# A two-layer diffusion backbone on one core: the instruction order is made by the framework's timeline simulation

## The chip, the cores and the metric

The kernel runs on one core of a Trainium2 chip. The metric is device time in microseconds (us) from the start to the end of one execution. The core has five engines that matter here, each with its own instruction queue: TensorE (PE; its weight loads are listed as PEld), VectorE (DVE), ScalarE (ACT), GpSimd (POOL) and SyncE (SP), which here only starts DMA transfers. An engine takes its queue in order and waits on semaphores for results of the others.

## What is computed

Two layers over 512 latent tokens and 256 context tokens of width 1024, all in fp32. Each layer has one input projection and three mixers side by side, then a projection back and an MLP:

```
h = rmsnorm(x) * (1 + scale) + shift
q, k, v, a, b, z, u, gate = split(h @ w_in)
o_na = neighbourhood_attention(q, k, v, kc, vc, rpb)     # 8 heads, softmax over window and context
o_dn = gated_head_norm(delta_f + delta_b, z)             # 4 heads, two directions, chunks
o_fn = real(fft2(u))                                     # 4 groups
y = (g_na * (o_na @ w_na_o) + g_dn * (o_dn @ w_dn_o) + g_fn * (o_fn @ w_fn)) @ w_out
x = x + gate1 * y
x = x + gate2 * (relu(rmsnorm(x) ... @ w1) ** 2 @ w2)
```

The delta rule solves a unit lower triangular system per chunk (`triangular_solve(I + strict_lower(beta k k^T * decay), rhs)`) and then carries a 128 x 128 state from chunk to chunk. In layer 1 the context tokens give only keys and values.

## The kernel before

**Stages.** A layer runs in three parts. First come norms, the Fourier mixer and the first delta head's inputs. Then comes the mix stage, in which the input projections, the attention and the delta rule run side by side (180.0 to 760.0 us in layer 0, 1658.8 to 2147.0 us in layer 1). Last comes the main stage: branch products, output projection, MLP (760.0 to 1540.0 us and 2147.0 us to the end); 1540.0 to 1658.8 us is the first part of layer 1.

**Projections.** `proj` (L250 to L256) makes every large product of fp32 weights as three products of halves: high weight with high input, high with low, low with high. All are recorded at L255, in 512 columns (`ps_in`) and 256 columns (`ps_inc`). `wload` (L235 to L248) brings 256 KB of weights (L240, a DMA issued on SP), takes their high half on ACT (L243) and the low half on DVE or POOL (L246); in the mix stages it is always POOL.

**Attention.** For each pair of heads and tile of 128 queries (`na_pair`): scores on PE (L841, L842), maxima, exponentials and sums on DVE and ACT (L806 to L819), the product with the reciprocal sum on DVE (L820), transposes on PE (L825), a copy on ACT (L826), products with V on PE (L831).

**Delta rule.** `l2_rope` (L484 to L507) takes the norm of keys and queries with a product against ones (L492) and turns them; `tok_major` (L509 to L517) transposes them (L515). `dn_prep` (L534 to L658) runs per head: six chunks of key products (L564) and query products (L566) give the tile `N`, whose diagonal blocks go out to DRAM (`nd`, L581, four DMAs) and come back as 48 blocks of 32 x 32 on 48 partitions (`Nb`, L583). Then DVE inverts them in 31 steps of a product (L591) and a subtraction (L593), each on the result of the last. L596 transposes; two DMAs write the result (L598, L599) and eight bring it back into `N` and `Tst` (L602, L603). Block products on PE then make the whole inverse (L612, L622, L638, L643). `dn_step` (L660 to L709) is one chunk of one direction of the recurrence, six per direction and head: L678 and L680 multiply with the state, L683 with the inverse, L685 copies the result on ACT, L687 makes the next state's product (added on DVE, L692), L705 the output's product (added on DVE, L703 to L709). `dn_out` (L720 to L738) norms a head's output (L729 on DVE) and transposes it (L735).

**What sets the order.** The program issues the mix stage through `by_clock`, which takes pieces of four streams (recurrence, `dn_prep`, attention, input projections) by a clock of rough costs and gives them priorities. The tile framework's scheduler then makes one order of all instructions, engine by engine, from the dependencies, the priorities and its own reckoning of times. The order is fixed when the program is built. Buffers limit it: `N`, `L` and the solve's scratch tile have one buffer each, so one head's inverse is in work at a time. The context that holds this scheduler is opened in `kernel` (L1359).

## Time and profile before

| | us |
|---|---|
| median of three timed runs | 2654.89 |
| the three runs | 2654.8, 2654.89, 2670.13 |
| the profiled execution | 2672.64 |
| its span, first to last instruction | 2670.7 |
| PE busy | 2481.4 (93%) |
| PE weight loads busy | 2046.0 (77%) |
| DVE busy | 1599.2 (60%) |
| ACT busy | 1187.1 (44%) |
| POOL busy | 645.8 (24%) |

The mean granted clock of TensorE is 0.974 of full speed. A matmul row's busy time holds its time in the pipe, so a busy share of PE over a stage says less than the spacing of its instructions. A wait is put down to the instruction whose semaphore came last. SPq rows are DMA issues in SP's queue, not transfers; the transfer ends later.

### The profile page before, as it was taken

To read this page: it belongs to the slowest core of one execution; us is meant where nothing else is said; L and a number is where in the kernel's file an instruction comes from. 1 tells how busy PE (TensorE), PEld (TensorE's weight loads), DVE (VectorE), ACT (ScalarE), POOL (GpSimd) and SP (SyncE) were. 2 spreads that over 40 slices of the span, in tenths; PEclk is the share of its full clock that TensorE was granted. 3 is DMA by queue.
4 is the path that set the end of the run, shared out by engine and by line. 5 is a ranking of instruction groups with operands and counts; after the bars stand their busy time and mean duration, and the time that the engine had idled before them with its cause. 6 is when DMAs were issued, how large, how long until landed. Compare 5 with 4: busy or idle time off the path is not lost. (4 is left out here: it accounts for less than half of the span.)

```text
span 2670.7 us, 39375 instructions
## 1 busy us (share of the span) xinstructions
PE 2481.4 (93%) x14608; PEld 2046.0 (77%) x14608; DVE 1599.2 (60%) x3207; ACT 1187.1 (44%) x2453; POOL 645.8 (24%) x536
## 2 busy tenths in 40 slices
PE   6988989899998999999999988888989999999998
PEld 3776877777887878888888867766767777788886
DVE  5647687768556967564434474868768456433334
ACT  4545545565564233131313264556555663423333
POOL 3231212231122122111111133222333232222222
PEclk8999999999999999999999999999989999999999
DMA  6232122222154643434343323223232346232332
GB/s 220 70 82 71 64 59 68 76 82 73 55 180 147 225 142 110 123 111 126 119 126 115 118 62 97 71 69 80 65 79 66 99 131 197 79 95 95 97 97 87
DMA packets 186247, 275.66 MB, mean 103 GB/s; under 512 B 57364, under 2 KB 77592, under 8 KB 185928
## 3 DMA queue, kind: packets, MB, share of 16 engines
q1 hardware_dynamic: 186056, 273.16, 33.8%
q8 instruction: 114, 1.87, 0.3%
q14 instruction: 77, 0.63, 0.1%
HBM read 242.86 MB, written 26.03 MB: 101 GB/s over the span
## 5 line engine op out<-in xcount | busy, mean ns | idle before, releaser
L246 POOL TENSOR_TENSOR wlo<-wr,whi 128x512 fp32r<-128x512 f32 x352 | 493.2, 1403 | 1666.8 <-ACT whi L243 1590.9
L243 ACT CAST whi<-wr 128x512 fp32r<-128x512 f32 x544 | 336.1, 619 | 794.8 <-PE ps_m L255 494.7
L255 PE MATMUL ps_in<-hh,whi 128*128 128x512 f32 x960 | 379.1, 406 | 15.5 <-ACT kraw L761 7.7
L255 PE MATMUL ps_in<-hh,wlo 128*128 128x512 f32 x960 | 375.4, 402 | 1.9 <-POOL wlo L246 1.9
L255 PE MATMUL ps_in<-hl,whi 128*128 128x512 f32 x960 | 376.8, 403 | 0.0
L255 PE MATMUL ps_m<-ml,whi 128*128 128x512 f32 (+1 forms) x768 | 234.2, 359 | 4.1 <-POOL ml L323 3.6
L255 PE MATMUL ps_m<-mh,whi 128*128 128x512 f32 (+1 forms) x768 | 232.2, 357 | 4.7 <-ACT mh L319 4.7
L255 PE MATMUL ps_m<-ah,wlo 128*128 128x512 f32 (+1 forms) x776 | 234.4, 355 | 0.0
L255 PE MATMUL ps_m<-al,whi 128*128 128x512 f32 (+1 forms) x776 | 233.1, 354 | 0.0
L255 PE MATMUL ps_m<-ah,whi 128*128 128x512 f32 (+1 forms) x776 | 233.0, 353 | 0.0
L255 PE MATMUL ps_m<-mh,wlo 128*128 128x512 f32 (+1 forms) x768 | 232.2, 356 | 0.0
L246 DVE TENSOR_TENSOR wlo<-wr,whi 128x512 fp32r<-128x512 f32 x192 | 134.7, 702 | 141.5 <-ACT whi L243 140.9
L255 PEld LDWEIGHTS ps_in<-hh,whi 128*128 128x128 f32 x960 | 181.4, 193 | 48.5 <-ACT kraw L761 8.1
L255 PEld LDWEIGHTS ps_in<-hh,wlo 128*128 128x128 f32 x960 | 180.0, 192 | 35.7 <-POOL wlo L246 3.2
L255 PEld LDWEIGHTS ps_in<-hl,whi 128*128 128x128 f32 x960 | 181.0, 193 | 30.3 <-issue 2.0
L1198 DVE SCALAR_TENSOR_TENSOR x<-ps_m,mod,x 128x512 f32<-128x512 f32 (+1 forms) x97 | 60.8, 654 | 217.9 <-PE ps_m L255 217.9
L202 DVE SCALAR_TENSOR_TENSOR jada<-wada,csb 128x1024 f32<-128x1024 f32 x128 | 179.1, 1399 | 1.2 <-DMA wada<-in_wat_dram 0.7
L255 PE MATMUL ps_inc<-hh,whi 128*128 128x256 f32 x512 | 150.9, 295 | 1.9 <-ACT gl L407 1.9
L255 PEld LDWEIGHTS ps_m<-ml,whi 128*128 128x128 f32 x768 | 127.7, 189 | 29.3 <-POOL ml L323 6.7
L255 PE MATMUL ps_inc<-hh,wlo 128*128 128x256 f32 x512 | 149.9, 293 | 0.0
L255 PE MATMUL ps_inc<-hl,whi 128*128 128x256 f32 x512 | 149.1, 291 | 0.0
L255 PEld LDWEIGHTS ps_m<-mh,whi 128*128 128x128 f32 x768 | 127.3, 189 | 27.7 <-ACT mh L319 6.4
(339 smaller groups left out, 5026.9 us busy)
## 6 DMA issues: line engine op xcount, KB each, us to landing
wr<-in_w_dram SPq DMA_DIRECT2D x256, 256.0 KB
wr<-in_wi_dram SPq DMA_DIRECT2D x224, 256.0 KB
wada<-in_wat_dram SPq DMA_DIRECT2D x80, 512.0 KB
wr<-in_wb_dram SPq DMA_DIRECT2D x48, 256.0 KB
wada<-in_wa_dram SPq DMA_DIRECT2D x32, 256.0 KB
wr<-in_wo_dram SPq DMA_DIRECT2D x32, 256.0 KB
gpre<-sgp SPq DMA_DIRECT2D x16, 384.0 KB
sgg<-gpre SPq DMA_DIRECT2D x16, 384.0 KB
```

What stands on the lines that cost most here:

```text
L202: pin(dve.scalar_tensor_tensor(junk, in0=ws[n], scalar=1.0, in1=cur["csb"][:, v * D:v * D + D], op0=ALU.mult, op1=ALU.mult, accum_out=MOD[ ...
L243: act.copy(hi, raw)
L246: eng.tensor_tensor(lo, raw, hi.bitcast(F32), op=ALU.subtract)
L255: pe.matmul(ps[:, s0 - off:s1 - off], lhsT=a, rhs=b[k][:, s0:s1], start=(k == 0 and i == 0), stop=(k == kn - 1 and i == 2))
L1198: dve.scalar_tensor_tensor(x2[k][:, s0:s1], in0=ps[:, s0:s1], scalar=mod(l, 5, k, v), in1=x2[k][:, s0:s1], op0=ALU.mult, op1=ALU.add)
```

## The change

One argument is given to the tile context. With it the scheduler makes the order of the instructions by its timeline simulation of the engines, where before it used its default reckoning of when each instruction can start. Nothing in the program's own code moves: the same instructions with the same tiles are in both, 12990 on PE, 3081 on DVE, 2271 on ACT, 541 on POOL and 1113 on SP.

```diff
     o = nc.dram_tensor("out_0_dram", (KD, P, TL), F32, kind="ExternalOutput").ap()
-    with tile.TileContext(nc) as tc:
+    with tile.TileContext(nc, schedule_with_timeline_sim=True) as tc:
         tile_backbone_kernel(tc, aps, o)
```

What it does to the order is seen at three places of PE's queue. The first is the second delta head of layer 0, around its last key and query products (L564, L566, tile `ps_kk_3040`). Before, projections of 256 columns (`ps_inc_3316`) stand around them:

```order
L255 MATMUL ps_inc_3316<-hl_260,whi_3281 128x256
L255 MATMUL ps_inc_3316<-hh_259,wlo_3282 128x256
L564 MATMUL ps_kk_3040<-kT_2353 128x128
L566 MATMUL ps_kk_3040<-qT_2891,kT_2353 128x128
L255 MATMUL ps_inc_3316<-hh_267,whi_3281 128x256
L255 MATMUL ps_inc_3316<-hl_268,whi_3281 128x256
L255 MATMUL ps_inc_3316<-hh_267,wlo_3282 128x256
```

In the change, the recurrence of the first head (`ps_ch`, with state `S` and inverse `L_2144`) stands behind them, its steps next to each other:

```order
L564 MATMUL ps_kk_3040<-kT_2353 128x128
L566 MATMUL ps_kk_3040<-qT_2891,kT_2353 128x128
L678 MATMUL ps_ch_2624<-S_2492,kT_585 128x128
L680 MATMUL ps_ch_2624<-S_2492,qT_985 128x128
L705 MATMUL ps_ch_2503<-Uc_2511,PT_1426 128x128
L683 MATMUL ps_ch_2624<-Z_2625,L_2144 128x128
L678 MATMUL ps_ch_2642<-S_2514,kT_585 128x128
L680 MATMUL ps_ch_2642<-S_2514,qT_985 128x128
L705 MATMUL ps_ch_2624<-Uc_2631,PT_1426 128x128
L683 MATMUL ps_ch_2642<-Z_2643,L_2144 128x128
L705 MATMUL ps_ch_2642<-Uc_2648,PT_1426 128x128
```

The projections have moved behind the recurrence, and the steps of its two directions are no longer apart.

The second place is the first block product L612 of the same head, which needs the inverse from the solve. Before, it stood among the attention's products with V, 349 matmuls behind the L564 above:

```order
L831 MATMUL ps_sc_4141<-Pm_4147,naV_3232 64x128
L831 MATMUL ps_sc_4141<-Pm_4154,naV_3232 64x128
L255 MATMUL ps_in_4268<-hl_276,whi_4258 128x512
L612 MATMUL ps_r_3397<-Tst_105,N_2908 32x32
L255 MATMUL ps_in_4268<-hh_275,wlo_4259 128x512
L255 MATMUL ps_in_4268<-hh_283,whi_4258 128x512
```

In the change it stands among projections of an earlier tile (`ps_in_3574`), 189 matmuls behind that L564:

```order
L255 MATMUL ps_in_3574<-hh_283,wlo_3565 128x512
L255 MATMUL ps_in_3574<-hh_399,whi_3570 128x512
L255 MATMUL ps_in_3574<-hl_400,whi_3570 128x512
L612 MATMUL ps_r_3397<-Tst_105,N_2908 32x32
L255 MATMUL ps_in_3574<-hh_399,wlo_3571 128x512
L255 MATMUL ps_in_3574<-hh_407,whi_3570 128x512
```

L612 has moved ahead of 160 matmuls. Over the eight heads the matmuls between the last L564 and the first L612 were 332, 349, 337, 328 in layer 0 and 338, 328, 355, 301 in layer 1; they are 306, 189, 347, 259 and 319, 235, 235, 161 in the change.

The third place is the transposes of the third head's output in layer 0 (L735, tiles `ps_ot_6971` and `ps_ot_6977`). Before, they stood among projections:

```order
L255 MATMUL ps_in_7019<-hh_283,wlo_7010 128x512
L255 MATMUL ps_in_7019<-hh_399,whi_7015 128x512
L735 MATMUL ps_ot_6971<-ident_432,O_6548 128x128 x4
L735 MATMUL ps_ot_6977<-ident_432,O_6548 128x128 x2
L255 MATMUL ps_in_7019<-hl_400,whi_7015 128x512
```

In the change they stand right behind the last output products (L705) of the head's recurrence:

```order
L683 MATMUL ps_ch_6943<-Z_6944,L_4970 128x128
L705 MATMUL ps_ch_6930<-Uc_6937,PT_4364 128x128
L705 MATMUL ps_ch_6943<-Uc_6949,PT_4364 128x128
L735 MATMUL ps_ot_6971<-ident_432,O_6548 128x128 x4
L735 MATMUL ps_ot_6977<-ident_432,O_6548 128x128 x2
L683 MATMUL ps_ch_6983<-Z_6986,L_6245 128x128
```

The projections between the last L705 and L735 have gone elsewhere. In the main stages PE's instructions keep their places but for one or a few.

## Rows read from the trace of the kernel before

**Rows 1.** Busy time by stage: us, busy us (x count), granted clock, DMA share, GB/s.

```profile
core 0: us, PE busy (x) PEld busy (x) DVE busy (x) ACT busy (x) POOL busy (x), PEclk, DMA share, GB/s
180.00:760.00 580.00, 532.93 (x3814) 440.26 (x3813) 394.48 (x1015) 331.26 (x773) 135.11 (x122) 0.97 0.26 73
760.00:1540.00 780.00, 764.06 (x4297) 663.08 (x4296) 454.00 (x664) 234.29 (x357) 145.90 (x100) 0.99 0.43 136
1658.80:2147.00 488.20, 433.41 (x2960) 342.22 (x2960) 347.68 (x905) 278.64 (x663) 140.02 (x117) 0.95 0.29 77
2147.00:2670.70 523.70, 504.91 (x2228) 408.61 (x2228) 231.53 (x326) 197.35 (x343) 130.97 (x101) 0.99 0.35 110
```

**Rows 2.** Waits of PE: us in total, times, longest us.

```profile
PE ps_s L825 <- DVE Pm L820: 30.7, 23, 6.9
PE ps_l L492 <- ACT r_l L487: 12.9, 9, 3.5
PE ps_kk L566 <- DVE qT L506: 7.1, 4, 3.0
PE ps_ot L735 <- DVE O L729: 4.7, 4, 3.0
```

**Rows 3.** Chain that ended last, then timeline of PE: start us, us, instruction, count.

```profile
2312.68 343.09 PE ps_m L255 x1501
...
223.11 0.28 PE L255 MATMUL ps_inc<-hh,wlo 128*128 128x256 f32 x1
223.23 0.29 PE L255 MATMUL ps_inc<-hh,whi 128*128 128x256 f32 x1
...
303.31 0.82 PE L735 MATMUL ps_ot<-ident,O 128*128 128x128 f32 x6
```

**Rows 4.** Timeline of the first head's inverse in layer 0, several engines.

```profile
179.93 0.38 PE L564 MATMUL ps_kk<-kT 128*128 128x128 f32 x2
180.15 0.28 PE L566 MATMUL ps_kk<-qT,kT 128*128 128x128 f32 x1
182.26 2.00 SPq L581 DMA_DIRECT2D nd<-N  x4
185.85 0.31 SPq L583 DMA_DIRECT2D Nb<-nd  x1
190.82 0.20 DVE L591 TENSOR_TENSOR stmp<-Nb,Wb 48x31 f32<-48x31 f32 x1 [6.48 <-DMA Wb<-in_eye_dram]
233.98 1.05 DVE L596 COPY Nb<-Wb 48x1024 f32<-48x1024 f32 x1
240.09 0.47 SPq L603 DMA_DIRECT2D Tst<-wd  x1
246.92 0.31 PE L612 MATMUL ps_r<-Tst,N 32*32 32x32 f32 x2
```

**Rows 5.** Busy time by window, last L564 to first L612: sum of eight.

```profile
sum 573.60, PE 509.91 PEld 403.49 DVE 462.79 ACT 320.60 POOL 139.08; mean PE 63.74 PEld 50.44 DVE 57.85 ACT 40.08 POOL 17.38
```

**Rows 6.** Busy time by window, first L591 to end of L596: sum of eight.

```profile
sum 372.90, PE 324.50 PEld 257.84 DVE 352.91 ACT 208.61 POOL 89.94; mean PE 40.56 PEld 32.23 DVE 44.11 ACT 26.08 POOL 11.24
```

**Rows 7.** Timeline of PE at the end of the last head, with idle time before.

```profile
2134.80 0.49 PE L705 MATMUL ps_ch<-Uc,PT 128*128 128x128 f32 x2 [0.74 <-DVE O L703]
...
2138.24 0.83 PE L735 MATMUL ps_ot<-ident,O 128*128 128x128 f32 x4 [2.95 <-DVE O L729]
```

**Rows 8.** Timeline of PE at a long wait, and busy time around it.

```profile
1831.21 0.45 PE L825 MATMUL ps_s<-ident,Pm 128*128 128x128 f32 x1 [6.91 <-DVE Pm L820]
...
1828.00:1834.80 6.80, 3.59 (x9) 2.16 (x10) 6.56 (x23) 4.06 (x9) 0.17 (x3) 0.50 0.03 9
```

**Rows 9.** All steps of the solve (ns min/median/max), then timeline of one step.

```profile
L591 DVE TENSOR_TENSOR stmp<-Nb,Wb x248: 170/357/1570, 190.8 to 2080.7; 48x31 f32<-48x31 f32 x8, 48x87 f32<-48x87 f32 x8, 48x135 f32<-48x135 f32 x8, 48x175 f32<-48x175 f32 x8
...
358.06 1.28 POOL L246 TENSOR_TENSOR wlo<-wr,whi 128x512 fp32r<-128x512 f32 x1 [10.05 <-ACT whi L243]
358.08 1.33 DVE L593 TENSOR_TENSOR Wb<-Wb,stmp 48x60 f32<-48x60 f32 x1
```

## The prediction

> **What bounds the kernel now.** I first read the busy time by stage [rows 1]. In the two main stages (branch products, output projection, MLP; 760 to 1540 us and 2147 us to the end) TensorE (PE) is busy for 764 of 780 us and 505 of 524 us; there it is the limit, and the new order moves its instructions by a place or so (up to three in the branch products), so I expect nothing from them. In the two mix stages, 180.0 to 760.0 and 1658.8 to 2147.0, PE is busy 533 of 580 us and 433 of 488 us, and no other engine comes near the span: DVE has 394 and 348 us. There PE loses time by standing in front of results that are not ready. The list of its waits [rows 2] shows who is late: the softmax (transposes L825 behind DVE, 30.7 us in 23 waits), the l2 norm (L492, 12.9 us), the queries after the rotary step (L566, 7.1 us), the delta output (L735, 4.7 us).
>
> A busy PE is not a working PE here, so I price its work by the spacing at which products follow each other when nothing waits: 1501 products of 512 columns in 343.09 us of the chain, 0.229 us each; 256 columns 0.12 us (223.11, then 223.23); 0.11 us for a transpose (six of one head end 0.82 us after the first starts, the last of them still some 0.27 in the pipe) [rows 3]; 0.22 us for an fp32 product of 128 columns (L564 at 179.93, L566 at 180.15) [rows 4]. Summed over the instruction order, the mix stages hold 467 and 368 us of PE work, 835 us in 1068 us: 233 us are lost to waits and to the low clock that follows them. All that the order can win or lose lies in there.
>
> **The change, part by part.** The same instructions with the same operands are issued; only their places on PE, DVE, ACT, POOL and in SP's queue move. I looked for what is placed closer to what it waits for, and what farther away.
>
> *Farther away, a gain.* Between the last scores of a softmax pair (L842) and its first transposes (L825) I price 4 to 6 us of PE work before and 6 to 9 us in the change (middle half, layer 0); between transposes and the products with V (L831) about 1 us before and 4 us now; ahead of L492 some 4 us more. So most of the 30.7 and 12.9 us of [rows 2] should go, where PE is not held by something else.
>
> *Closer, a loss.* The delta branch inverts a triangular matrix per head: the products L564 give N; N goes to DRAM and comes back with 48 blocks on the partitions (L581, L583); DVE runs 31 dependent steps (L591, L593); the result makes the same way back (L598 to L603); then PE goes on at L612. It occurs eight times, four heads in two layers. Before, the priced PE work between a head's last L564 and its first L612 was 52.9, 53.3, 52.1, 51.2 us in layer 0 and 58.7, 56.4, 63.6, 56.6 us in layer 1, together 445 us. In the change it is 49.0, 32.8, 55.0, 40.2 and 55.0, 42.4, 43.0, 32.7 us, together 350 us (the order of the second head is shown above). PE takes its queue strictly in order, so after this work it has to stand at L612 until the chain is through.
>
> How long is that chain? The eight stretches from the last L564 to the first L612 took 573.6 us [rows 5], that is 129 us of PE loss inside them. The solve itself, from the first L591 to the copy L596, took 372.9 us, with DVE busy for 352.9 of them, 95% [rows 6]: it is bound by DVE. The DVE instructions that stand there sum to 407.6 us by their own durations (they overlap a little, so time is 0.915 of the sum); in the change those that stand between the same two instructions sum to 398.9 us by the same durations, so 365 us. The two ends of the chain are transfers. In the first head [rows 4] L564 is at 179.93, N goes out from 182.26, comes back with the read at 185.85, first L591 at 190.82: 10.9 us (10.8 to 15.4 over the eight). At the other end L596 ends at 235.03, two writes and eight reads follow, the last issued at 240.09, L612 at 246.92: 11.9 us (9.5 to 15.8). PE shows no wait at L612 before, so the far end may hold slack: the four writes of N are issued until 184.26, the read behind them at 185.85, 1.6 us for a landing; with that the far end needs 240.09 + 0.47 + 1.6 - 235.03 = 7.1 us. So the two ends cost 18 us a head at least, and 25.1 us as they were ((573.6 - 372.9) / 8); I take 20.5 us, nearer the lower end, because a PE that waits takes the result the moment it lands. The chain is then 365 + 8 x 20.5 = 529 us (509 to 566).
>
> PE loss inside the eight stretches: 529 - 350 = 179 us against 129 us now, +50 us (+30 to +87). The gains of the softmax inside these stretches are not counted again: PE only reaches L612 earlier and stands there longer.
>
> The 95 us of PE work that left the stretches now lie outside them: 835 - 350 = 485 us, where 390 us took 1068 - 574 = 494 us, a loss of 104 us. What changes there:
> - The steps of the delta recurrence are placed back to back where the order before had projections between them. A hop with nothing in it left PE idle for 0.74 us (L705 at 2134.80, [rows 7]); the other direction's products still stand in most of them, so I put 0.3 us on each of some 60 hops, +18 us.
> - L735 right behind L705: uncovered it cost 2.95 us [rows 7]. Before, only the last head had it so; now five do, and a sixth with 0.55 us between. Two of the new ones lie outside the stretches, +6 us.
> - The queries of the second head come 4.1 us of PE work after their norm, where 11.6 us were needed, +7 us.
> - Softmax, norm and transposed keys outside the stretches, -15 us; block products L638 and L643, placed farther apart, -6 us.
> - After a wait the granted clock is 0.5 for a stretch: from 1828.0 to 1834.8, behind the wait of 6.91 us at L825 [rows 8], which costs half the work of the stretch, 3.4 us. Eight longer waits at L612 against smaller ones that vanish: I take +2 us net.
> Together +12 us, between -40 (more filler covers more) and +40.
>
> The stages before and between the mixes have the first weights and norms as their limits, and their distances change by 1 to 3 us of PE work either way: 0, give or take 10 us. SP's queue keeps the solve's transfers close together, with one or two weight loads ahead of them as before: 0.
>
> Sum: 50 + 12 = +62 us on the span of 2670.7 us. That profiled execution took 2672.64 us, near the slowest of the three timed runs (2654.8, 2654.89, 2670.13); added to the median it gives 2717 us, 2.3% more.
>
> **Rivals.**
> *The wait is repaid* (no change, about 2660 us). The +50 us comes true, but 95 us of moved projections cover the outside so well that its 104 us fall by 45. For it: every long chain (L492, L515, L825, L842) stands farther from its source. Against it: the outside loss is mostly recurrence and block products, and the recurrence is placed closer. Chance 0.20, with chains of 509 us and half the repayment counted in.
>
> *The solve gets shorter* (faster, about 2617 us). A step of the solve takes 0.36 us in the middle, 0.17 at the shortest, but up to 1.57 us; the 60-element one at 358.08 took 1.33 us, beside a POOL subtraction of 1.28 us from 358.06 [rows 9]. Over all 496 steps their own time is 207 us; with every step at the shortest of its size it would be 160 us. If a waiting PE also holds back POOL's weight splits so that this goes away, the chain is 482 us, the loss inside 132 us, and with -40 outside the result is -37 us. It decides where the chain falls under 490 us, 61 us a head. Against it: the weight splits must still be done, and POOL runs ahead of PE only by its buffers.
> The Trainium skill (GPSIMD Engine Reference, section 1. Specifications) says that POOL's SBUF interfaces are shared with VectorE, with contention when a DVE instruction has two SBUF inputs; the row of 1.33 us agrees. The Trainium skill (DMA: Bandwidth & Descriptors, Anatomy of one DMA) puts about 2 us of fixed cost on a DMA, mostly the receipt of its last write; the 1.6 us behind the issue is near it. By that figure alone four hops cost 8 us a head, an estimate: a chain of 429 us, a loss inside of 79 us and the side of this rival; the rows show 18 us and more, because the four and eight transfers of a hop are issued one after another.
> Chance of this rival 0.12.
>
> *The chain stays as slow as it was* (slower, about 2780 us): 25.1 us at the ends, 566 us, +87, and +40 outside for the recurrence. For it: the spread of both ends. Chance 0.20.
>
> *The order does nothing* can only be so in the main stages; in the mixes nearly every PE instruction has another place.
>
> **Chances and range.** The forecast, between 2682 and 2760 us, has 0.48. Slower by over 1% (about what a measurement of this kernel tells from no change) is this and the slow chain, 0.68; within 1% 0.20; faster 0.12. The range for 8 in 10 goes from 2640, which takes in the repaid case, to 2780.
>
> **What would show it.** Right: PE waits at L612 appear in its list, some 5 to 25 us each and over 60 us together, the longest at the second head of layer 0 and the last of layer 1; DVE stays over 90% busy in the solves; waits at L825 and L492 fall below half; main stages unchanged within 5 us. Wrong: no wait at L612 (the chain was shorter), or waits there with mix stages no longer than 1068 us (repaid).

## The result, and the profile after

The changed kernel takes 2737.02 us (median of 4 runs, 2734.98 to 2740.6); the kernel before takes 2660.72 us beside it (4 runs, 2654.8 to 2670.13). The ratio is 1.0269, with a 95% interval of 1.0247 to 1.029: 2.7% slower. The prediction was 2717 us, with 2640 to 2780 as its range. The profiled execution took 2734.98 us, its span 2733.2 us.

First the busy time by stage of the changed kernel, cut where its own stages begin (us, then busy us and count by engine, granted clock, DMA share, GB/s). It answers to [rows 1]:

```profile
core 0: us, PE busy (x) PEld busy (x) DVE busy (x) ACT busy (x) POOL busy (x), PEclk, DMA share, GB/s
194.00:790.00 596.00, 525.09 (x3730) 443.89 (x3728) 404.49 (x1014) 323.54 (x762) 136.71 (x119) 0.93 0.24 68
790.00:1567.00 777.00, 763.06 (x4296) 663.25 (x4296) 458.15 (x668) 234.67 (x358) 141.68 (x100) 0.99 0.43 138
1702.10:2210.40 508.30, 439.99 (x2887) 356.74 (x2886) 355.60 (x904) 270.84 (x650) 131.90 (x113) 0.89 0.25 72
2210.40:2733.20 522.80, 502.76 (x2229) 407.68 (x2227) 238.74 (x325) 196.96 (x344) 132.59 (x102) 0.99 0.35 110
```

The main stages are what they were (777 for 780 us, 523 for 524 us). The mix stages hold fewer PE instructions than before (3730 for 3814, 2887 for 2960; the others now run ahead of them) and still take 16 and 20 us longer. The granted clock in them fell from 0.97 to 0.93 and from 0.95 to 0.89. The stages ahead of the mixes grew by 14 and 16 us, with about as much more work in them.

The waits of PE in the changed kernel (us in total, times, longest), beside [rows 2]:

```profile
PE ps_s L825 <- DVE Pm L820: 22.3, 12, 4.4
PE ps_ot L735 <- DVE O L729: 20.9, 5, 5.5
PE ps_ch L705 <- DVE O L701: 8.8, 8, 3.5
PE ps_ch L705 <- DVE O L703: 7.0, 14, 0.9
PE ps_r L612 <- DMA Tst<-wd: 6.8, 7, 1.9
PE ps_l L492 <- ACT r_l L487: 5.3, 3, 2.7
```

Softmax and norm lost waits, the output transposes L735 grew from 4.7 to 20.9 us, the recurrence's L705 came in with 15.8 us. L612, on which the prediction's largest term rested, waits for 6.8 us in all, in four of the eight heads; in the other four PE comes to it when the result has landed.

Then the eight stretches from a head's last L564 to its first L612, and the solves in them (first L591 to the end of L596), as sums of eight windows, beside [rows 5, 6]:

```profile
sum 495.80, PE 418.72 PEld 345.72 DVE 414.86 ACT 253.10 POOL 115.53; mean PE 52.34 PEld 43.22 DVE 51.86 ACT 31.64 POOL 14.44
...
sum 370.00, PE 311.98 PEld 257.67 DVE 344.45 ACT 196.81 POOL 77.59; mean PE 39.00 PEld 32.21 DVE 43.06 ACT 24.60 POOL 9.70
```

The solves are as long as before (370.0 for 372.9 us, DVE 93% busy). The two ends of the chain shrank from 25.1 to (495.8 - 370.0) / 8 = 15.7 us a head. With 350 us of priced PE work in 495.8 us, PE loses 146 us there, against 130 before.

**Where the time went.** I priced PE's work as in the prediction and took it from the time between the same landmarks in both traces (loss = time - work, us, from PE's first instruction to its last; the last two columns are experiments told below):

| stretch | before: time, loss | change: time, loss | loss, a_free | loss, b_free |
|---|---|---|---|---|
| start to last L564 of head 0 | 166.3, 35.5 | 179.7, 33.3 | 34.4 | 34.4 |
| eight stretches L564 to L612 | 574.6, 129.7 | 496.2, 146.0 | 139.3 | 127.1 |
| L612 to the next head's last L564, or to the layer's last L645 | 383.3, 89.1 | 481.2, 102.5 | 101.7 | 77.1 |
| last L645 to the branch products, both layers | 110.9, 15.2 | 126.8, 49.9 | 21.5 | 6.0 |
| start of layer 1 to last L564 of its head 0 | 116.2, 23.7 | 135.0, 28.8 | 28.3 | 24.0 |
| main stages | 1297.1, 51.8 | 1289.4, 44.0 | 46.5 | 51.3 |
| sum | 2648.4, 345.0 | 2708.4, 404.5 | 371.6 | 319.9 |

Of the 60 us more loss, 35 lie in the two short tails behind the last inverse of each layer, 16 in the eight stretches (all of it in the last two heads of layer 1: 15.9 to 24.6 and 13.9 to 22.3 us), 13 around the block products.

A tail in rows (a tail is the stretch from a layer's last L645 to its branch products): PE at the output transposes of the third head of layer 0, in the changed kernel (start us, us, instruction, idle before and its releaser). Before, the same L735 stood among projections and waited for nothing; those rows of the kernel before stand first.

```profile
695.35 0.39 PE L255 MATMUL ps_in<-hh,wlo 128*128 128x512 f32 x1
695.58 0.39 PE L255 MATMUL ps_in<-hh,whi 128*128 128x512 f32 x1
695.81 0.82 PE L735 MATMUL ps_ot<-ident,O 128*128 128x128 f32 x6
696.38 0.47 PE L255 MATMUL ps_in<-hl,whi 128*128 128x512 f32 x1
```

```profile
709.33 0.49 PE L705 MATMUL ps_ch<-Uc,PT 128*128 128x128 f32 x2 [0.93 <-DVE O L703]
713.77 1.54 PE L735 MATMUL ps_ot<-ident,O 128*128 128x128 f32 x6 [3.95 <-DVE O L729]
715.73 0.80 PE L683 MATMUL ps_ch<-Z,L 128*128 128x128 f32 x2 [0.42 <-DVE o_dn L736]
...
717.76 0.63 PE L255 MATMUL ps_in<-hh,wlo 128*128 128x512 f32 x1
718.19 0.63 PE L255 MATMUL ps_in<-hh,whi 128*128 128x512 f32 x1
...
719.15 0.40 PE L255 MATMUL ps_in<-hh,whi 128*128 128x512 f32 x1
719.38 0.40 PE L255 MATMUL ps_in<-hl,whi 128*128 128x512 f32 x1
```

The wait of 3.95 us is one loss. Another follows it: products of 512 columns start 0.43 us apart (717.76, 718.19), and only later 0.23 us apart (719.15, 719.38). The stretch from 711.9 to 718.7 us has a granted clock of 0.5 (the first row; the two below it are other such stretches). At the end of the same tail the branch products L1101 wait 6.0 us for ACT.

```profile
711.90:718.70 6.80, 4.51 (x15) 3.65 (x16) 2.30 (x4) 3.36 (x13) 0.00 (x0) 0.50 0.16 61
769.90:776.80 6.90, 3.70 (x14) 3.32 (x15) 2.96 (x4) 4.51 (x17) 0.00 (x0) 0.51 0.08 33
2159.20:2179.70 20.50, 17.29 (x174) 14.19 (x174) 5.09 (x17) 12.56 (x33) 0.00 (x0) 0.50 0.16 58
```

Over both mix stages the time short of the full clock is 0.03 x 580 + 0.05 x 488 = 42 us before and 0.07 x 596 + 0.11 x 508 = 98 us in the change, from the stage rows. PE was idle in a part of it; counted only between instructions that follow without a gap, the low clock cost by these prices about 37 us before and 72 us in the change, and the gaps themselves 102 and 139 us. The Trainium skill (TensorE: Matmul & The Clock Gate, What's actually happening) puts the cost of the ramp under 1% of a typical kernel's span. That is the ramp at a kernel's start; here the low clock comes back behind waits all through the mix stages, and it costs 1.4% of the span before and 2.6% in the change.

### The profile page after: what moved, and what is told of

It reads as the page before. It is cut to its first block, busy times and chain, and to the rows that moved or that the text cites. A ratio compares the mean times of both kernels' runs of the same rounds, so it can differ in the third digit from the quotient of the medians.

```text
span 2733.2 us, 39393 instructions
## 1 busy us (share of the span) xinstructions
PE 2503.9 (92%) x14608; PEld 2089.3 (76%) x14608; DVE 1629.6 (60%) x3207; ACT 1183.6 (43%) x2453; POOL 642.6 (24%) x536
## 4 chain that ended last, share of the span: by engine, by line
PE 64%; DVE 12%; DMA 6%; ACT 3%; issue 2%; SPq 1%; POOL 1%; DVEq 0%; ACTq 0%; POOLq 0%
PE ps_m L255 32%; PE ps_in L255 13%; PE ps_wo L255 4%; PE ps_br L255 3%; PE ps_inc L255 3%; DVE stmp L591 2%; DVE Wb L593 1%; DMA Db<-gdr 1%; DMA Wb<-in_eye_dram 1%; DVE xn L313 1%; DVE cy L478 1%; PE ps_s L831 1%; PE ps_s L825 1%; PE ps_br L1101 1%; PE ps_ch L683 1%
## 5 line engine op out<-in xcount | busy, mean ns | idle before, releaser
L246 DVE TENSOR_TENSOR wlo<-wr,whi 128x512 fp32r<-128x512 f32 x192 | 145.7, 759 | 136.0 <-ACT whi L243 135.1
L255 PEld LDWEIGHTS ps_m<-al,whi 128*128 128x128 f32 x776 | 127.7, 187 | 23.6
```

The lines of the kernel that those rows point to most:

```text
L246: eng.tensor_tensor(lo, raw, hi.bitcast(F32), op=ALU.subtract)
L255: pe.matmul(ps[:, s0 - off:s1 - off], lhsT=a, rhs=b[k][:, s0:s1], start=(k == 0 and i == 0), stop=(k == kn - 1 and i == 2))
```

## The experiments

Several kernels fix the order of one or all engines' queues. Their code is the same but for this, with the list of instructions written into the file; the edges order the issue on one engine and add no wait:

```diff
         tile_backbone_kernel(tc, aps, o)
+        for a, b in zip(order, order[1:]):
+            tc.add_manual_dep(by[b], a, mybir.DependencyInfo(mybir.DependencyClass.NoSync, ...), reason="order")
```

**One engine's order from each kernel.** Is it PE's order that carries the time? In one kernel PE has the order of before and the simulation orders the other engines; in the other PE has the order of the change and the default reckoning orders the rest. So the other queues are those of neither kernel; they are made anew around PE's (of DVE's instructions about two thirds keep the order of before in the first, and three quarters that of the change in the second).

> PE keeps the order of before, instruction for instruction; the four other queues are ordered by the timeline simulation around it. Three theories. Inverse (the first block product L612 comes too early for the solve): only PE's order matters, 2645 to 2680 us. Recurrence (the hops between L678, L683, L687, L705 and the output transposes L735 are less covered by other products): only PE's order matters, 2645 to 2680 us. Other queues (the same PE order would do, but DVE and ACT serve the wrong thing first): 2700 us or more.

> PE has the order of the change, instruction for instruction; the four other queues are ordered by the default reckoning around it. Inverse and recurrence theory: the loss sits in PE's order and stays, 2715 to 2755 us. Other queues: below 2690 us.

Measured: 2762.88 us (ratio 1.038, 1.0346 to 1.0414) and 2792.72 us (1.0492, 1.0458 to 1.0526). Both are slower than both kernels. The second lies outside what any of the theories gave, and the first falls on the side of the other queues. In the second, PE now does wait at L612 (us in total, times, longest):

```profile
PE ps_r L612 <- DMA Tst<-wd: 31.5, 10, 9.7
PE ps_ot L735 <- DVE O L729: 23.0, 6, 4.6
```

So the same PE order waits 6.8 us at L612 with the queues that were made beside it, and 31.5 us with others. An order of PE has no time of its own; what it costs is settled by the orders of DVE, ACT and SP that stand against it. The prediction priced its largest term from PE's order; of the other queues it used DVE's in the solve and SP's around the transfers.

**The inverse moved up in the order of before.** This makes one part of the change and little else, the part that the prediction put at +50 us: the block products stand as close behind the last L564 as in the change.

> The order of before, but the block products L612 to L645 moved up, so that between a head's last L564 and its first L612 stands the PE work of the change (349 us over eight heads instead of 443). The other queues by the default reckoning. Theory of the inverse, as in the prediction: PE comes to L612 before the solve is through and waits, +15 to +50 us, 2675 to 2710 us. Theory of the serial head: the chain from L564 to L612 loses its slack of 3 to 10 us a head, L645 and the next head's keys come earlier, 15 to 30 us faster, 2630 to 2645 us.

Measured: 2761.44 us (ratio 1.0369, 1.033 to 1.0407), 96 us more, past the upper end of the first theory; the second falls. The waits of PE are the ones that the prediction described:

```profile
PE ps_r L612 <- DMA Tst<-wd: 71.5, 6, 16.5
PE ps_s L825 <- DVE Pm L820: 26.0, 20, 6.9
PE ps_l L492 <- ACT r_l L487: 18.3, 9, 7.9
```

The stretches take 515.7 us and hold 349 us of work, a loss of 167 us for 130 before: +37. The rest of the loss lies outside them, most of it between L612 and the next head's L564, and the clock has a large part in it. These are the two mix stages (same columns as the stage rows):

```profile
178.60:806.30 627.70, 552.86 (x3816) 457.20 (x3815) 390.39 (x1015) 334.79 (x774) 133.82 (x122) 0.92 0.23 68
1703.20:2238.50 535.30, 437.11 (x2961) 348.26 (x2960) 347.30 (x905) 278.55 (x663) 141.77 (x117) 0.91 0.25 70
```

The clock is short by 0.08 x 628 + 0.09 x 535 = 98 us there, for 42 before; from L612 to the next head's L564, or to the layer's last L645, it stood at 0.5 for 117 us, for 45 before. So bringing L612 closer does cost time when little else in PE's order has moved with it, and behind the long waits as well as in them. In the change most of these waits stood elsewhere; that the other moves of the order did this is my reading.

**The inverse moved back in the order of the change.** The opposite part, made by the simulation itself under one rule more. It makes the rest of the order anew too (about a fifth of DVE's instructions stand in another order than in the change), so it isn't this part alone:

```diff
+        for late, early in LATE:      # L612 of heads 0, 1, 3 to 6; a projection product of the same head's stretch
+            tc.add_manual_dep(by[late], early, mybir.DependencyInfo(mybir.DependencyClass.NoSync, ...), reason="order")
```

> The timeline simulation makes the order as in the change, with one rule more: L612 of heads 0, 1, 3, 4, 5 and 6 may not be issued on PE before a projection product that stands as far behind the head's last L564 as L612 stood before. PE work between them is 395 us over the eight heads (349 in the change, 443 before). Theory of the balance: 47 us of work stand beside the solves again, 15 to 40 us come back, 2697 to 2722 us. If the place of L612 is not what costs, 2732 to 2745 us; if L612 then delays the next head, over 2750 us.

Measured: 2725.13 us (ratio 1.0229, 1.0203 to 1.0256), 12 us less than the change, between what the balance gave and what no effect would give; the intervals of the two ratios overlap, so the size is uncertain. The waits at L735 stayed (22.4 us in 5). The balance would have taken the gain inside the eight stretches, but they take 539 us with 395 us of work in them, a loss of 144 us for 146 in the change; the gain lies behind L612. So the 12 us can't be put down to the place of L612, and no run shows what that place is worth in the order of the change.

**The block products closer together.** In the change L612 to L645 takes 30 to 37 us for heads 0, 1, 2, 4, 5 and 6, where it took 14 to 24 us before, and the next head's L564 follows it, since `N` has one buffer.

> The order of the change, but the block products L612, L622, L638, L643 of heads 0 to 6 stand as close together on PE as before (12 to 14 us of PE work from the first to the last, where the change had 20 to 27). The other queues are ordered by the timeline simulation around it. Theory of the serial head (N has one buffer, so a head's keys L564 wait for the last block product of the head before it, and this chain, not PE, sets the mix stages): L612 to L645 took 31 to 38 us for heads 4 to 6 and 30 to 32 us for heads 0 to 2, and 15 to 24 us before; with it 30 to 60 us come back, 2677 to 2707 us. Theory of covered waits (PE's own waits add up): the products now have less between them, 2735 to 2745 us.

Measured: 2775.63 us (ratio 1.0417, 1.0384 to 1.045), 39 us slower than the change; both theories fall. L612 to L645 did get shorter (36.1 to 23.4 us and 37.3 to 25.5 us for heads 5 and 6), but the way to the next head's last L564 grew by as much (29.7 to 43.1 and 29.4 to 46.6 us), because those products now had the projections in front of them. From one head's L645 to the next it was 132.6 and 134.5 us in the change and is 131.2 and 136.6 us here. PE now waits for the copies between the block products:

```profile
PE ps_ot L735 <- DVE O L729: 22.4, 5, 5.9
PE ps_s L825 <- DVE Pm L820: 18.3, 11, 3.4
...
PE ps_r L638 <- ACT R L640: 14.0, 5, 7.1
```

**A short solve, in both orders.** All five queues are fixed; each step works on one element:

```diff
-                n, m = 31 - j, j + 1
+                n, m = 1, 1
```

> All five queues in the order of before. Changed: each of the 62 steps of a solve works on one element instead of up to 256, so the solve is short and the inverse is wrong. Theory of the serial head: the solves of layer 1 take some 20 us instead of 49, and PE follows as far as its own work lets it: layer 1's mix stage falls from 488 us to 410 to 440 us, layer 0's by 10 to 40 us, the whole to 2550 to 2600 us. Theory of covered waits: PE's waits at L825, L492, L515 stay, only DVE's share in them falls, 2625 to 2655 us.

> All five queues in the order of the change; each of the 62 steps of a solve works on one element (the inverse is wrong), as in the kernel of the same kind in the order of before, which took 2625.5 us, 40 us off. Theory of the balance: in the order of the change too little PE work stands beside the solve on DVE, so PE idles there; with the solve's own work gone it gives back more than before did, the stretches from L564 to L612 fall from 496 us to 430 to 450 us and the time by 50 to 75 us, to 2662 to 2687 us. Theory of the hops: the waits are in the recurrence and in the output transposes and hang on DVE only as far as it is busy, 25 to 45 us come back, 2692 to 2712 us.

Measured, one run each: 2625.51 us in the order of before, 40 us under the median of 2665.64 beside it, and 2710.61 us in the order of the change, 26 us under the 2737.02 of the change. So the first time lies at the lower end of what covered waits gave, and the second near the upper end of what the hops gave; the serial head's 2550 to 2600 us and the balance's 2662 to 2687 us fall. The steps' own time fell from 207 to 114 us in the order of before. The stretches fell from 574.6 to 538.0 us there and from 495.8 to 466.8 us in the order of the change, so the solve is on the path that sets the time. But it isn't what sets the two orders apart: 85 us lie between them with short solves, 76 without. The solve as a whole shrank far less than its steps (372.9 to 335.1 us), since the other instructions that stand between them in DVE's queue now wait for ACT (36 us over the eight solves, 6 before) and for PE (21 us, 6 before). The sum of the eight solves in the order of before:

```profile
sum 335.10, PE 313.03 PEld 253.94 DVE 269.42 ACT 206.08 POOL 76.67; mean PE 39.13 PEld 31.74 DVE 33.68 ACT 25.76 POOL 9.58
```

DVE is 80% busy there. My reading of [rows 6], "bound by DVE", was half of it: with DVE relieved, what ACT and PE bring to its queue is the next limit, 10% away.

**Less work for DVE.** The product L820 moves from DVE to ACT, in the kernel before. The default reckoning makes the order anew for it (about a quarter of DVE's instructions change places), so the new order is tried along with the lighter DVE:

```diff
-                dve.tensor_scalar(Pm[:, :nk], Pm[:, :nk], s4[:, 5:6], None, op0=ALU.mult)
+                act.activation(out=Pm[:, :nk], in_=Pm[:, :nk], func=AF.Copy, scale=s4[:, 5:6])
```

> The kernel before, with the default reckoning; the product with the reciprocal sum (L820, 0.47 us each on DVE, 72 of them) is done on ACT instead. If DVE bounds the solves (95% busy there) and with them the mix stages, 10 to 25 us come back, 2635 to 2655 us; ACT has 57% in the mix stages. If PE's own waits bound them, 2650 to 2675 us, since the softmax chain gets no shorter.

Measured: 2665.04 us (ratio 1.0005, 0.9985 to 1.0024): no difference, as the theory of PE's own waits had it. The wait at L825 fell from 30.7 to 18.3 us (now behind ACT), that at L492 rose from 12.9 to 22.9 us.

**Hops taken away, in both orders.** Are the recurrence and the output transposes what the change lost on? A first pair of kernels replaced only PE's operands.

> All five queues in the order of the change. Changed: the products of the recurrence (L678, L680, L683, L687, L705) read the value tile or the identity instead of the state S, the tile Z and the copy Uc, and the output transposes L735 read the identity instead of O, so that none of them has to wait for a hop on DVE or ACT, and the delta branch computes something else. Recurrence theory: in the mix stages these lines lost 81 us (hops) and 30 us (L735) against spacing; some 20 us may remain as waits for PSUM tiles, so the time falls by 70 to 100 us to 2635 to 2665 us. Inverse theory: PE reaches L612 earlier and waits there instead, the time falls by less than 30 us.

> The same replaced operands in the order of before, all five queues. Recurrence theory: these lines lost 34 us and 6 us, so the time falls by 15 to 40 us, to 2620 to 2645 us, and what is left between this kernel and the one in the order of the change is under 30 us of the 72. Inverse theory: some 50 us or more are left between the two.

Measured: 2729.01 us and 2658.66 us (one run each), 8 us less than the change and 1 us less than before. The edit did less than it said. PE still waited for DVE's and ACT's reads of the PSUM tile that it writes:

```profile
PE ps_ch L705 <- DVE O L701: 8.3, 8, 3.4
PE ps_ch L705 <- DVE O L703: 7.2, 14, 0.9
PE ps_ch L687 <- ACT Uc L685: 5.9, 15, 0.4
```

Only the wait at L735 had gone. That gives a result of its own: 20.9 us of waits removed in the change brought back 8 us, for L825 behind DVE rose from 22.3 to 32.4 us and L1101 behind ACT, at the end of a tail, from 6.0 to 12.3 us. The second pair replaced the readers' operands too, so that neither side waits:

```diff
-            pe.matmul(ps[:, P:2 * P], lhsT=lhs, rhs=v_t, start=True, stop=True)
+            pe.matmul(ps[:, P:2 * P], lhsT=lhs, rhs=ident, start=True, stop=True)
-            act.copy(Uc, ps[:, P:2 * P])
+            act.copy(Uc, ident)
```

> All five queues in the order of the change. Changed: in the recurrence PE's products read the identity instead of S, Z and Uc, and DVE and ACT read the identity instead of the products' PSUM tile, so that neither side waits for the other there; the output transposes L735 read the identity. The delta branch computes something else; as many instructions of the same sizes run. The kernel with only PE's operands replaced kept its hop waits, since PE still waited for the readers of the PSUM tile; only L735's wait had gone, for 8 us. Theory of the hops: L678 to L705 lose 81 us against their spacing here and 34 us in the order of before, L735 30 and 6; with all of it gone the time falls by 50 to 100 us, to 2637 to 2687 us. Theory of repayment (a wait taken away in one place comes back at the next result that is late, the softmax or L612): it falls by 10 to 35 us, 2702 to 2727 us.

> The same replacement in the order of before. Theory of the hops: 15 to 35 us come back, 2625 to 2650 us, and between this kernel and the one in the order of the change under 40 of the 72 us are left. Theory of repayment: 0 to 15 us, 2645 to 2665 us, and 50 us or more are left.

Measured: 2705.04 us (ratio 1.0162, 1.014 to 1.0184) and 2647.25 us (0.9936, 0.9914 to 0.9957), 32 and 13 us less; 58 us are left between the two orders, 60 by the ratios, where there were 76 and 72. The theory of repayment holds: against their spacing the lines L678 to L705 and L735 lost 111 us in the change and 24 us here, but the waits came back at the next results that were late:

```profile
PE ps_s L825 <- DVE Pm L820: 26.8, 12, 4.9
PE ps_tm L515 <- DVE kT L506: 19.0, 3, 10.4
PE ps_in L255 <- ACT zz L407: 14.6, 1, 14.6
```

All gaps of PE in the mix stages together are 139 us in the change and 145 us here. Two things came back instead. The time lost to the low clock fell from about 72 to 55 us. And in the tails less was left to wait for: of the 33 us less loss in the table, 28 lie there. In the tail of layer 0 PE waits 18.5 us in the change and 12.6 us here, all of it in two waits; in that of layer 1 it waits 5.7 us in the change and not at all here:

```profile
PE ps_br L1101 <- ACT obh L262: 8.0, 1, 8.0
PE ps_ch L683 <- DVE o_dn L736: 4.6, 1, 4.6
```

The tails, from the last L645 of layers 0 and 1 to the branch products, in this kernel (beside 91.4 and 35.0 us with a clock of 0.91 and 0.84 in the change, 73.5 and 36.9 us with 1.00 and 0.95 before):

```profile
697.80:775.60 77.80, 65.11 (x417) 58.15 (x413) 29.70 (x84) 41.95 (x106) 9.73 (x9) 0.94 0.20 70
2155.60:2175.80 20.20, 20.15 (x142) 18.26 (x138) 14.32 (x49) 13.37 (x45) 1.68 (x2) 0.92 0.14 47
```

Not tried: L735 or the recurrence moved behind projections in the order of the change. The next projection needs a PSUM tile of the two that projections share, and a gate projection already there (its `zz` tile is freed by L736, behind L735) holds one until L735 has run, so by the program such an order would block; no run shows it.

## Why the prediction held, and which of its steps did not

The time (2737 for 2717 us) and the sign came out, and the spans of the two profiled executions differ by 62.5 us, as forecast. By the medians the difference is 76 us, 14 more. That it came so near is luck in part: two terms of the sum were wrong, and their errors cancelled.

- *Main stages unchanged:* right, within 3 us.
- *The length of the chain from L564 to L612:* 496 us for 529, under the lower end of 509. The solve was right (370 for 365 us). The ends were mis-sized: 15.7 us a head, where I had 18 as the least and took 20.5. In the four heads in which PE waits at L612 it starts 5.0 to 5.9 us behind the end of L596, and in the four in which PE comes late 6.1 to 8.3 us. My bound of 7.1 us let L612 wait for the last of the eight reads. The last head of the change shows that it doesn't: the first L612 starts 0.44 us behind the issue of that read, and it is the next ones that wait for a later landing.

```profile
2148.78 2.22 DVE L596 COPY Nb<-Wb 48x1024 f32<-48x1024 f32 x1
...
2155.53 0.47 SPq L603 DMA_DIRECT2D Tst<-wd  x1
...
2155.97 0.24 PE L612 MATMUL ps_r<-Tst,N 32*32 32x32 f32 x2 [1.12 <-DMA Tst<-wd]
...
2157.53 0.38 PE L612 MATMUL ps_r<-Tst,N 32*32 32x32 f32 x12 [0.72 <-DMA Tst<-wd]
```

- *PE loss inside the stretches, +50 us:* it was +16. In the prediction's own sum (chain less 350 us of work) the miss is that of the chain above. The direction is right, and the experiment b_612, which makes this move nearly alone, shows the mechanism with 71.5 us of waits at L612, in six heads. In the change itself the sign that I named, waits of 60 us and more at L612, is not there (6.8 us): PE lost the time on its way, at L735, L705 and L825, and came to L612 when the result was about to land or had landed. So two steps failed: the size of the chain's ends, and that PE arrives at L612 after 350 us of work with nothing else in its way.
- *Outside, +12 us:* it was +48, past the upper bound of 40: 13 around the block products and 35 in the tails. (The other stages, which I put at 0, gave back 5.) Its parts: the recurrence hops lost 81 us against their spacing where it had been 34, +47 for my +18; L735 lost 30 for 6, +24 for my +6 (not all of both lies outside the stretches). L492 did fall by more than half (12.9 to 5.3 us), L825 did not (30.7 to 22.3 us). The block products cost more, not less: "L638 and L643 placed farther apart" was booked as a gain of 6 us.
- *The clock, +2 us:* the term with the largest error. By the prices it was about +35 us (37 to 72), spread over the stretches and the rest, so it is a part of both terms above. I had the mechanism, from [rows 8], and put against each other the long waits that come and those that go. What the change brought was many more stretches at 0.5 (25 in the mix stages for 15), behind single waits of 1 to 6 us and behind trains of short hops. The +2 us were also too little for what they were meant for: in b_612, with its six long waits at L612, the clock is short by 98 us for 42 before.
- *The rivals:* "the wait is repaid" described most of what the experiments did. L735's wait gone gave back 8 of 21 us, hops and L735 gone gave back 32 of 87 us, and L820 moved gave nothing. It did not end at no change: what the last pair got back lies mostly in the tails, and in the time at the low clock. "The solve gets shorter" did not happen: 200 us of own steps for 207.

What is settled: PE's order alone does not decide it (pe_before and pe_after); the solve's length does not set the two orders apart (the short solves); the hops and L735 together account for 12 to 18 of the 72 to 76 us (the last pair), mostly in the tails; a_late brought 12 us back, but not in the stretches, and with the rest of the order made anew. What stays open is some 45 to 60 us of the difference, the larger part. The trace shows where they lie, the last two heads of layer 1, the block products, the low clock behind many small waits; no run took them away singly, and no kernel that does the whole computation came out under the one before.

## What to carry to other kernels

A wait that is removed off the end of a stage was mostly repaid here at the next late result; count it in full only where little follows that could wait, in the tail of a stage. A wait that is added is not repaid in the same way: 71.5 us at L612 in the order of before cost 96 us. An engine's order has no price of its own: both kernels, each ordered as a whole, were faster than those with PE's order kept and the rest made anew, so an edit by hand to one queue has to be followed through the others. And where TensorE's clock falls behind waits, price the slow products after the wait as well as the wait.

## What the runs showed of the hardware

The granted clock of PE at its lower level cost about as much as the waits that came with it: in the mix stages of the change the clock was short by 98 us in sum, for 42 before, some 35 us of it between instructions without a gap, while the gaps of PE grew by 37 us. Stretches at 0.5 also came where no single wait was long: from 2159.2 to 2179.7 us PE ran mostly block products, transposes, scores and products with V, with gaps of at most 1.8 us, and its longest gap just ahead of that was 1.1 us (at L612). The round trip over DRAM at the far end of the chain (two writes, eight reads) let the first L612 start 5.0 us after the copy L596 in the fastest head, where the rows of before had led me to 7.1 us as the least.
